# A chunk inverse whose first transposed step is made by a mask on VectorE

## The chip, the cores and the metric

The kernel runs on one core of a Trainium2 chip. The metric is the device time of one execution in microseconds (us), the median of the runs shown. PE is the matrix engine (TensorE), PEld its weight loads, DVE is VectorE, ACT is ScalarE, POOL is GpSimd, and SP issues the weight transfers. Times in the rows are counted from the start of the profiled span.

## The reference, cut to what matters

One inference step of a two-layer decoder trunk runs over 512 prompt tokens and 8 samples of 8 tokens. Each layer has a mixer (one combined input projection; a gated delta rule with 4 heads of 128, a pooling and a short convolution read it), an output projection, and a gated MLP. In the delta rule each chunk of tokens needs a triangular solve:

```
a = einsum('bhnid,bhnjd->bhnij', kb, k) * where(strict, decay, 0)
sol = lax.linalg.triangular_solve(eye + a, rhs, left_side=True, lower=True)
u, w = sol[..., :dv], sol[..., dv:]
```

The kernel takes four chunks of 128 prompt tokens (0 to 3) and one block-diagonal chunk of 64 rows for all samples (chunk 4), and builds the inverse of `eye + a` for all 4 heads of a chunk.

## The kernel before, in words

Tokens stand in the free dimension (576 of them, in two halves of 288 columns), features on partitions. A dense matmul multiplies a 128x128 weight piece by one half. Each fp32 product is made of three matmuls of rounded parts (`xh` by `whi`, `xl` by `whi`, `xh` by `wlo`); ACT makes `whi` from the loaded `wraw`, DVE makes `wlo`. The input projection of a layer has 24 groups of 48 dense matmuls, 1152 in all; this text counts places on PE by how many of them have gone before. The delta rule runs inside the projection, between its dense matmuls, from the 444th on.

The order is written once, when the program is built. Generators (`tri`, `delta`, `sample`, `vtrans` and the tails of each group) are advanced by a planner that keeps an estimated clock for each engine; `tick`, after each three dense matmuls, advances those whose estimated front has passed. `aside` marks work on which the generator's front does not wait. On the chip every engine then runs its own list in that order and waits on semaphores. `room(2)`, at the start of each group, advances generators until at most two tails still hold a PSUM bank. The pooling tails wait for `vtrans`, the transposes of V, so that at place 864, the start of the group after the two pooling groups, the planner writes out all that `vtrans` needs and whatever comes up meanwhile, with no dense matmul between.

`tri` inverts a chunk. Two streams of it run side by side: stream 0 has chunks 0 and 2, stream 1 has 1, 4 and 3. It builds `A` (fp32) from the cumulated gates `gc` and the products of K (`KQ` rows on PE), its fp16 copies `Ah` and `Al`, and the factor `E`. Then it doubles the inverse, 7 steps for 128 rows and 3 for 64. `UT[:, :, 0]` is the inverse so far, `UT[:, :, 1]` its transposed form. A step s multiplies `Ah` with the inverse (P, 4 matmuls), masks P by level s (H, one DVE operation), multiplies H with the transposed form both ways (Y, 8 matmuls in two PSUM banks) and copies both banks with ACT. In step 0 the inverse is the identity, so P is a transpose through `identr`. Two refinement rounds and the product with Q follow.

In rows `m` and `m_149` to `m_152` are the four memory regions that hold these tiles: `UT` of stream 0 lies in `m_151`, that of stream 1 and `Ah`, `Al`, `H` in `m_152`, `A` and `U` in `m_149`. A row `ps<-m` or `ps<-m,m` with f16 is a matmul of `tri`; `vs<-ps,c` is ACT copying a V transpose, `cv`, `pad` and `VZ<-th,cv` are the convolution tails of K, Q and V.

Of the kernel before, what the change touches and what calls it, by code (L numbers as in the profile page):

```python
# [10 lines left out]
F16 = mybir.dt.float16  # L11
I32 = mybir.dt.int32
AF = mybir.ActivationFunctionType
ALU = mybir.AluOpType
# [8 lines left out]
NH = 4  # L23
# [16 lines left out]
    _C[_n] = (_o, _o + _w)  # L40
    _o += _w
NCONST = _o
NLEV = 7 * 128
_P = {}
_o = 0
for _n, _w in (("gmix", 8), ("gffn", 8), ("gfin", 8), ("cw", 48), ("alog", 20), ("dtb", 20), ("onorm", 1),
# [6 lines left out]
def _levels():  # L53

    i = np.arange(128)
    lev = np.zeros((128, 7, 128), np.float32)
    for n in range(7):
        b = i >> n
        lev[:, n] = np.eye(128) - ((b[:, None] // 2 == b[None, :] // 2) & (b[:, None] % 2 == 0) & (b[None, :] % 2 == 1))
    return lev.reshape(128, NLEV)  # L60


def _constants():
    c = np.zeros((128, NCONST + NLEV), np.float32)
    c[:, NCONST:] = _levels()

    def put(n, a):
        a = np.asarray(a, np.float32)
        c[:a.shape[0], _C[n][0]:_C[n][0] + a.shape[1]] = a

    i = np.arange(128)
    put("ident", np.eye(128))
    put("ones", np.ones((128, 2)))
    put("tu", i[:, None] <= i[None, :])
    s = np.arange(64)
    blk = (s[:, None] // ST) == (s[None, :] // ST)
    put("tus", blk & (s[:, None] <= s[None, :]))
    put("bones", blk)
    put("mx", np.where(i[:, None] > i[None, :], -1e30, 1e4))
    put("my", np.where(i[None, :] >= i[:, None], 1e30, -1e4))  # L80
    put("mxs", np.where(blk & (s[:, None] > s[None, :]), -1e30, 1e4))
    put("mys", np.where(blk & (s[None, :] >= s[:, None]), 1e30, -1e4))
    put("bmask", (s[:, None] // ST) == np.arange(8)[None, :])
    put("sel", np.tile(np.eye(8), (2, 1)))
    win = np.repeat(np.array([[2, 4], [8, 16]]), 64, axis=1).T
    put("winv", 1.0 / win)
    put("wsel", np.repeat(np.array([[0, 1], [0, 1]]), 64, axis=1).T)
    pos = np.arange(15)
    put("ptab", np.concatenate([1.0 / np.minimum(pos[None, :] + 1, win[:, t:t + 1]) for t in range(2)], axis=1))
    return c  # L90
# [150 lines left out]
class _Trunk:  # L241
# [933 lines left out]
    def tri(self, l, par, chunks):  # L1175

        nc, V, S = self.nc, self.nc.vector, self.nc.scalar

        def tl(name, dt=F32):
            return self.carve(f"{name}{par}", (NH, 128), dt)  # L1180

        for c in chunks:
            n = 128 if c < 4 else 64
# [3 lines left out]
            idr = self.identr[0:n, 0:n]  # L1187
# [7 lines left out]
            def grid(p=n):  # L1195
                return self.psum()[0:p, 0:NH * n].rearrange("p (h i) -> p h i", i=n)
# [23 lines left out]
            with self.aside():  # L1220
                if c < 4:
                    V.tensor_copy(ekv, B[:, :, 127:128])
                    V.tensor_tensor(out=ek[:, NH:2 * NH], in0=ek[:, 0:NH], in1=self.gc[:, 4 * c:4 * c + NH],
                                    op=ALU.subtract)
# [15 lines left out]
            Ah = tl("Ah", F16)[0:n, :, 0:n]  # L1240
# [14 lines left out]
            lev = self.lev[0:n]  # L1255
            UT = self.carve(f"UT{par}", (NH, 2, 128), F16)[0:n, :, :, 0:n]
            for s in range(7 if c < 4 else 3):
                P = grid()
                for h in range(NH):
                    self.mm(P[:, h], Ah[:, h], idr if s == 0 else UT[:, h, 0])  # L1260
                H = UT[:, :, 0] if s == 0 else tl("H", F16)[0:n, :, 0:n]
                V.tensor_tensor(out=H, in0=P, in1=lev[:, s:s + 1, 0:n].to_broadcast([n, NH, n]), op=ALU.mult)
                self.back(P)
                yield
                if s == 0:
                    Y = grid()
                    for h in range(NH):
                        self.mm(Y[:, h], H[:, h], idr)
                    S.activation(out=UT[:, :, 1], in_=Y, func=AF.Copy)
                    self.back(Y)  # L1270
                else:
                    for j in (0, 2):
                        Y = self.psum()[0:n, 0:4 * n].rearrange("p (h u i) -> p h u i", u=2, i=n)
                        for i in range(2):
                            self.mm(Y[:, i, 0], UT[:, j + i, 1], H[:, j + i])
                            self.mm(Y[:, i, 1], H[:, j + i], UT[:, j + i, 1])
                        with self.aside():
                            S.activation(out=UT[:, j:j + 2], in_=Y, func=AF.Copy)
                            self.back(Y)
                yield  # L1280

            if c in (2, 3):
                yield lambda: len(self.chunks) > c - 2 and self.chunks[c - 2]
# [4 lines left out]
            for it in range(2):  # L1288
                P = grid()
                for h in range(NH):  # L1290
                    self.mm(P[:, h], Ah[:, h], C[:, h], stop=False)
                    self.mm(P[:, h], Al[:, h], C[:, h], start=False)
                F = tl("H", F16)[0:n, :, 0:n]
# [319 lines left out]
    def build(self):  # L1613
        nc, tc, ctx, a = self.nc, self.tc, self.ctx, self.a
        V, S = nc.vector, nc.scalar
# [57 lines left out]
        nc.gpsimd.dma_start(out=self.const[:, c0:], in_=a["consts"][:, c0:NCONST])  # L1673
        levels = [self.temp("lev") for _ in range(2)]
        self.free["tmp"] -= 2
        for j, (s0, s1) in enumerate(((0, 4), (4, 7))):
            nc.gpsimd.dma_start(out=levels[j][:, 0:128 * (s1 - s0)],
                                in_=a["consts"][:, NCONST + 128 * s0:NCONST + 128 * s1])

        def halve():  # L1680

            self.lev = self.pc.tile([128, 7, 128], F16, name="lev")
            V.tensor_copy(self.identr, self.c("ident"))
            for j, (s0, s1) in enumerate(((0, 4), (4, 7))):
                V.tensor_copy(self.lev[:, s0:s1], levels[j][:, 0:128 * (s1 - s0)].rearrange("p (s i) -> p s i", i=128))
            self.give(*levels)

# [24 lines left out]
        for l in range(L):  # L1712
            name, _, groups = next(ph)
# [437 lines left out]
```

## Time and profile before

| | us |
|---|---|
| median of 3 runs (1498.53 to 1500.83) | 1499.11 |
| the profiled execution's own time | 1498.7 |
| its span | 1496.9 |

The span is from the first to the last instruction; 1.8 us lie around it. PE is busy for 1467.6 us of the span, so little of it is spent waiting, and what waits there are can be listed one by one.

### The profile page before, as it was taken

How to read it: one execution, taken by the hardware profiler on the slowest of the kernel's cores; microseconds unless marked ns; L12 is line 12 of the kernel's file. 1: busy time of each engine (PE TensorE's matmuls, PEld its weight loads, DVE VectorE, ACT ScalarE, POOL GpSimd, SP SyncE). 2: the span in 40 equal slices, each digit the busy share in tenths (PEclk: the TensorE clock that was granted, in tenths of full speed). 3: DMA queues.
4: the chain of work that ended last, by engine and by line, in shares of the span. 5: the costliest groups of instructions: out<-in, count | busy, mean ns of one | idle time of the engine just before them, and what ended most of it. 6: DMA issues, size and time to landing. Idle time of an engine off the chain costs nothing.

```text
span 1496.9 us, 29634 instructions
## 1 busy us (share of the span) xinstructions
PE 1467.6 (98%) x11462; PEld 1430.1 (96%) x11462; DVE 1072.3 (72%) x2381; ACT 670.2 (45%) x1427; POOL 186.9 (12%) x636
## 2 busy tenths in 40 slices
PE   9999999999999999999999999999999999999997
PEld 7999899899999999999999988989999999999997
DVE  7887776668748786478667887766595678854865
ACT  6345565544433343144434546755343334432442
POOL 3211023401000010001121111242010001000100
PEclk9999999999999999999999999999999999999999
DMA  6121122332232323222422112025222232232222
GB/s 199 58 63 44 48 75 86 129 103 78 85 92 86 99 72 92 85 93 73 144 75 70 58 43 90 26 86 174 78 78 79 84 102 82 85 92 92 72 84 85
DMA packets 67278, 128.78 MB, mean 86 GB/s; under 512 B 7952, under 2 KB 13248, under 8 KB 67136
## 3 DMA queue, kind: packets, MB, share of 16 engines
q1 hardware_dynamic: 59808, 105.15, 22.7%
q0 software_dynamic: 6208, 20.56, 3.8%
q8 instruction: 90, 1.47, 0.4%
q10 hardware_dynamic: 1120, 1.18, 0.2%
q14 instruction: 52, 0.43, 0.1%
HBM read 116.36 MB, written 10.49 MB: 85 GB/s over the span
## 4 chain that ended last, share of the span: by engine, by line
PE 87%; issue 5%; DVE 4%; POOL 2%; ACT 1%; DMA 1%; SPq 0%; POOLq 0%; DVEq 0%; ACTq 0%
PE ps L458 75%; PE q L458 10%; PE ps L229 2%; DVE m L229 1%; DMA xr<-in_x_dram 1%; ACT m L229 1%; DVE cv L229 1%; DVE wlo L229 0%; DVE sqacc L229 0%; POOL kr_t L229 0%; POOL os_t L229 0%; POOL qr_t L229 0%; ACT whi L229 0%; POOL o_y L229 0%; DVE xl L229 0%
## 5 line engine op out<-in xcount | busy, mean ns | idle before, releaser
L229 DVE TENSOR_TENSOR wlo<-wraw,whi 128x512 fp32r<-128x512 f32 (+1 forms) x428 | 285.7, 677 | 84.1 <-ACT whi L229 82.6
L229 ACT ACTIVATE whi<-wraw 128x512 fp32r<-128x512 f32 (+1 forms) x428 | 257.1, 615 | 147.3 <-PE ps L458 122.1
L458 PE MATMUL ps<-xh,whi 128*128 128x288 f32 x768 | 243.7, 317 | 0.1
L458 PE MATMUL ps<-xl,whi 128*128 128x288 f32 x768 | 227.1, 296 | 0.5 <-DVE xl L229 0.5
L458 PE MATMUL ps<-xh,wlo 128*128 128x288 f32 x768 | 226.4, 295 | 0.4 <-DVE wlo L229 0.4
L458 PE MATMUL ps<-hh,whi 128*128 128x288 f32 x704 | 208.5, 296 | 0.0
L458 PE MATMUL ps<-hl,whi 128*128 128x288 f32 x704 | 207.6, 295 | 0.0
L458 PE MATMUL ps<-hh,wlo 128*128 128x288 f32 x704 | 207.0, 294 | 0.0
L458 PE MATMUL ps<-nh,whi 128*128 128x288 f32 x640 | 189.3, 296 | 0.0
L458 PE MATMUL ps<-nl,whi 128*128 128x288 f32 x640 | 188.8, 295 | 0.0
L458 PE MATMUL ps<-nh,wlo 128*128 128x288 f32 x640 | 188.2, 294 | 0.0
L458 PEld LDWEIGHTS ps<-xh,whi 128*128 128x128 f32 x768 | 144.7, 188 | 5.8 <-issue 2.4
L458 PEld LDWEIGHTS ps<-xl,whi 128*128 128x128 f32 x768 | 144.9, 189 | 1.5 <-DVE xl L229 1.1
L458 PEld LDWEIGHTS ps<-xh,wlo 128*128 128x128 f32 x768 | 144.5, 188 | 0.9 <-DVE wlo L229 0.9
L458 PEld LDWEIGHTS ps<-hh,wlo 128*128 128x128 f32 x704 | 132.6, 188 | 0.0
L458 PEld LDWEIGHTS ps<-hl,whi 128*128 128x128 f32 x704 | 132.2, 188 | 0.0
L458 PEld LDWEIGHTS ps<-hh,whi 128*128 128x128 f32 x704 | 131.9, 187 | 0.0
L458 PEld LDWEIGHTS ps<-nh,wlo 128*128 128x128 f32 x640 | 120.5, 188 | 0.0
L458 PEld LDWEIGHTS ps<-nl,whi 128*128 128x128 f32 x640 | 120.1, 188 | 0.0
L458 PEld LDWEIGHTS ps<-nh,whi 128*128 128x128 f32 x640 | 119.9, 187 | 0.0
L229 POOL COPY fs<-gpad 128x2 f32<-128x2 f32 x88 | 30.7, 365 | 677.2 <-DVE gpad L229 604.5
L229 DVE SCALAR_TENSOR_TENSOR xr<-ps,xr 128x288 f32<-128x288 f32 x96 | 41.2, 457 | 99.5 <-PE ps L458 99.1
(312 smaller groups left out, 3354.3 us busy)
## 6 DMA issues: line engine op xcount, KB each, us to landing
wraw<-in_w_gu_dram SPq DMA_DIRECT2D x176, 256.0 KB, 2.8
wraw<-in_w_in_dram SPq DMA_DIRECT2D x96, 256.0 KB, 2.7
wraw<-in_w_dn_dram SPq DMA_DIRECT2D x80, 256.0 KB, 2.7
wraw<-in_w_out_dram SPq DMA_DIRECT2D x32, 256.0 KB, 2.9
xr<-in_x_dram POOLq DMA_DIRECT2D x12, 288.0 KB, 5.3
vs<-in_st_delta_dram POOLq DMA_DIRECT2D x6, 512.0 KB, 4.4
out_s_delta_dram<-vs POOLq DMA_DIRECT2D x6, 512.0 KB, 3.1
spill<-xr POOLq DMA_DIRECT2D x8, 288.0 KB, 2.5
```

The source lines that it names most:

```text
L229: return f(*args, **kw)
L458: self.nc.raw.tensor.matmul(out, lhsT, rhs, start=start, stop=stop)
```

## The change: the diff and the new order

A further level, `lev[:, 7]`, is the transpose of level 0. In step 0 the change makes `UT[:, :, 1]`, which was the transpose of the masked H, directly as `Ah` times this level, by one DVE operation on fp16 from SBUF. The four second transposes, the PSUM bank they took and ACT's copy go, and with them the `yield` that followed. The constants grow by 128 columns, which come with the second of two transfers.

```
     for n in range(7):
         ...
+    lev[:, 7] = lev[:, 0].T
...
                 P = grid()
+                if s == 0:
+                    with self.aside():
+                        V.tensor_tensor(out=UT[:, :, 1], in0=Ah, in1=lev[:, 7:8, 0:n].to_broadcast([n, NH, n]),
+                                        op=ALU.mult)
                 for h in range(NH):
                     self.mm(P[:, h], Ah[:, h], idr if s == 0 else UT[:, h, 0])
                 H = UT[:, :, 0] if s == 0 else tl("H", F16)[0:n, :, 0:n]
                 V.tensor_tensor(out=H, in0=P, in1=lev[:, s:s + 1, 0:n].to_broadcast([n, NH, n]), op=ALU.mult)
                 self.back(P)
                 yield
-                if s == 0:
-                    Y = grid()
-                    for h in range(NH):
-                        self.mm(Y[:, h], H[:, h], idr)
-                    S.activation(out=UT[:, :, 1], in_=Y, func=AF.Copy)
-                    self.back(Y)
-                else:
+                if s:
                     for j in (0, 2):
...
-                yield
+                    yield
```

Since the planner's clocks see other costs, the order of the whole mixer changes in both layers. The first place is DVE in layer 0, where chunks 0 and 1 end (`m_150<-ps,m_149` is their product with Q) and chunks 2 and 4 begin (`ps,gc`). Before, from place 711 on PE:

```order
L229 TENSOR_TENSOR m_149<-m_149,ps 128x512
L229 TENSOR_TENSOR m_149<-m_152 128x512
L229 TENSOR_TENSOR m_152<-m_150,ps 128x512
L229 TENSOR_TENSOR m_150<-ps,m_149 128x512
L229 TENSOR_TENSOR m_149<-m_149,ps 128x512
L229 SCALAR_TENSOR_TENSOR m_149<-ps,gc,consts 128x128 x4
L229 COPY ek<-ps 128x4
L229 TENSOR_TENSOR ek<-ek,gc 128x4
L229 TENSOR_TENSOR m_150<-ps,m_149 128x512
L229 SCALAR_TENSOR_TENSOR m_149<-ps,beta,m_149 128x128 x4
L229 TENSOR_TENSOR m_149<-m_149,consts 128x512
L229 SCALAR_TENSOR_TENSOR m_149<-ps,gc,consts 64x64 x4
```

Now, from place 768 to 777:

```order
L230 TENSOR_TENSOR m_149<-m_149,ps 128x512
L230 SCALAR_TENSOR_TENSOR cv<-pad,prm_91,cv 128x600 x3
L230 TENSOR_TENSOR pad<-ps,rn 128x288
L230 TENSOR_TENSOR pad<-ps,rn 128x224
L230 TENSOR_TENSOR pad<-ps,rn 128x8x8
L230 TENSOR_TENSOR wlo_2130<-wraw_1820,whi_2129 128x512
L230 TENSOR_TENSOR m_149<-m_149,ps 128x512
L230 TENSOR_TENSOR m_150<-ps,m_149 128x512 x2
L230 SCALAR_TENSOR_TENSOR m_149<-ps,gc,consts 128x128 x4
L230 COPY ek<-ps 128x4
L230 TENSOR_TENSOR ek<-ek,gc 128x4
L230 SCALAR_TENSOR_TENSOR m_149<-ps,gc,consts 64x64 x4
```

A convolution, a group's evacuation and a weight split now stand ahead of the beginning of chunk 2, and that beginning has moved 66 dense matmuls later. On PE the first transpose of chunk 2 moves from place 750 to 813, that of chunk 4 from 786 to 864.

The second place is ACT in layer 0 at place 864, where the V transposes are copied (`vs<-ps,c`) between the copies of the doubling steps (`m_151<-ps` for chunk 2, `m_152<-ps 64x4x64` for chunk 4). Before:

```order
L229 ACTIVATE m_152<-ps 64x4x64 x2
L229 ACTIVATE m_151<-ps 128x512 x2
L229 ACTIVATE m_152<-m_150 64x4x64
L229 ACTIVATE vs<-ps,c_1007 64x128 x4
L229 ACTIVATE m_152<-ps 64x4x64
L229 ACTIVATE m_151<-ps 128x512 x2
L229 ACTIVATE vs<-ps,c_1007 128x128 x4
L229 ACTIVATE m_151<-ps 128x512 x2
L229 ACTIVATE vs<-ps,c_1007 128x128 x8
L229 ACTIVATE m_149<-m_149 128x512
L229 ACTIVATE ek<-ek 128x8
L229 ACTIVATE m_151<-ps 128x512 x2
```

Now:

```order
L230 ACTIVATE vs<-ps,c_1007 64x128 x4
L230 ACTIVATE m_151<-ps 128x512 x2
L230 ACTIVATE m_152<-ps 64x4x64 x2
L230 ACTIVATE vs<-ps,c_1007 128x128 x4
L230 ACTIVATE m_151<-ps 128x512 x2
L230 ACTIVATE m_152<-ps 64x4x64 x2
L230 ACTIVATE vs<-ps,c_1007 128x128 x4
L230 ACTIVATE m_152<-m_150 64x4x64
L230 ACTIVATE m_151<-ps 128x512 x2
L230 ACTIVATE vs<-ps,c_1007 128x128 x4
L230 ACTIVATE m_152<-ps 64x4x64
L230 ACTIVATE m_151<-ps 128x512 x2
```

Chunk 2 now has its first five doubling steps' Y products in this stretch, where it had four of later steps, and chunk 4 has both its doubling steps and its refinement there. Layer 1 has the same order as layer 0 in both places.

## Rows read from the trace of the kernel before

**Rows 1.** The page, parts 1 and 4: busy time of each engine; the chain's shares.

```profile
PE 1467.6 (98%) x11462; PEld 1430.1 (96%) x11462; DVE 1072.3 (72%) x2381; ACT 670.2 (45%) x1427; POOL 186.9 (12%) x636
...
PE 87%; issue 5%; DVE 4%; POOL 2%; ACT 1%; DMA 1%; SPq 0%; POOLq 0%; DVEq 0%; ACTq 0%
```

**Rows 2.** Timeline, PE: start, duration, engine, line, operation, shapes, [idle before].

```profile
143.68 0.38 PE L458 MATMUL ps<-m 128*128 128x128 f16 x4 [1.27 <-ACT m L229]
...
282.98 0.40 PE L458 MATMUL ps<-ol,whi 128*128 128x288 f32 x1 [1.25 <-DVE ol L229]
...
869.90 0.61 PE L458 MATMUL ps<-m 128*128 128x128 f16 x8 [0.52 <-DVE m L229]
...
880.97 0.38 PE L458 MATMUL ps<-m 128*128 128x128 f16 x4 [1.70 <-ACT m L229]
```

**Rows 3.** Stretches: length, busy PE, PEld, DVE, ACT, POOL; clock, DMA, GB/s.

```profile
175.20:187.80 12.60, 9.75 (x117) 8.19 (x116) 7.79 (x22) 10.22 (x30) 0.00 (x0) 1.00 0.02 6
...
912.40:925.10 12.70, 9.85 (x119) 8.22 (x117) 7.90 (x23) 10.22 (x30) 0.00 (x0) 1.00 0.03 10
```

**Rows 4.** Groups by form, PE, ACT and DVE: count, busy us, mean ns, idle.

```profile
L458 PE MATMUL ps<-identr,m 128*128 128x128 f16 x64 | 6.3, 221 | 0.0
...
L229 ACT ACTIVATE m<-ps 128x512 f16<-128x512 f32 x112 | 60.0, 599 | 33.9 <-PE ps L458 33.9
...
L229 ACT ACTIVATE m<-ps 64x256 f16<-64x256 f32 x12 | 4.1, 375 | 6.6 <-PE ps L458 4.0 <-issue 2.6
...
L229 DVE TENSOR_TENSOR m<-ps,lev 128x512 f16<-128x512 f32 x56 | 37.9, 686 | 10.1 <-PE ps L458 9.9
```

**Rows 5.** Tile lev: the casts of the levels, ns min, median, max.

```profile
L229 DVE CAST lev<-lev x2: 352/385/418, 28.5 to 28.8; 128x512 f16<-128x512 f32 x1, 128x384 f16<-128x384 f32 x1
```

**Rows 6.** Timeline, PE: a group of 4 and one of 8 between dense matmuls.

```profile
134.81 0.29 PE L458 MATMUL ps<-xh,wlo 128*128 128x288 f32 x1
...
134.95 0.40 PE L458 MATMUL ps<-m 128*128 128x128 f16 x4
...
135.37 0.30 PE L458 MATMUL ps<-xl,whi 128*128 128x288 f32 x1
...
137.21 0.29 PE L458 MATMUL ps<-xh,wlo 128*128 128x288 f32 x1
...
137.35 0.62 PE L458 MATMUL ps<-m 128*128 128x128 f16 x8
...
137.99 0.30 PE L458 MATMUL ps<-xl,whi 128*128 128x288 f32 x1
```

**Rows 7.** Timeline around the beginning of chunk 2, PE, DVE and ACT.

```profile
131.87 1.28 DVE L229 TENSOR_TENSOR m<-ps,lev 128x512 f16<-128x512 f32 x2
...
133.67 2.60 DVE L229 SCALAR_TENSOR_TENSOR cv<-pad,prm,cv 128x600 f32<-128x600 f32 x3
...
146.82 1.06 PE L458 MATMUL ps<-KQ 128*128 128x128 f32 x8
...
148.74 1.12 DVE L229 SCALAR_TENSOR_TENSOR m<-ps,gc,consts 128x128 f32<-128x128 f32 x4
...
154.50 0.61 ACT L229 ACTIVATE m<-m 128x512 f16<-128x512 f32 x1
```

**Rows 8.** Timeline inside the stretch at place 864.

```profile
175.04 1.56 DVE L229 SCALAR_TENSOR_TENSOR VZ<-th,cv 128x512 f32<-128x512 f32 x4
...
176.48 0.69 PE L229 MATMUL ps<-consts,VZ 128*64 128x128 f32 x4
...
178.29 0.61 PE L458 MATMUL ps<-m,m 128*128 128x128 f16 x8 [0.47 <-DVE m L229]
...
180.90 0.61 PE L458 MATMUL ps<-m,m 128*128 128x128 f16 x8 [0.41 <-DVE m L229]
...
181.38 1.08 ACT L229 ACTIVATE m<-ps 128x512 f16<-128x512 f32 x2 [0.55 <-PE ps L458]
182.35 1.15 ACT L229 ACTIVATE vs<-ps,c 128x128 f32<-128x128 f32 x4
```

**Rows 9.** Stretches of 1 us in layer 0, the clock behind POOL's time.

```profile
124.00:125.00 1.00, 1.00 (x11) 0.97 (x11) 0.98 (x6) 0.87 (x2) 0.00 (x0) 0.74 0.00 0
...
126.00:127.00 1.00, 1.00 (x12) 1.00 (x12) 1.00 (x3) 0.36 (x1) 0.00 (x0) 0.50 0.00 0
127.00:128.00 1.00, 1.00 (x10) 1.00 (x9) 1.00 (x4) 1.00 (x3) 0.00 (x0) 0.55 0.00 0
```

More of the change, by code (lines that the diff above doesn't have):

```diff
@@ L42 @@
 NCONST = _o
-NLEV = 7 * 128
+NLEV = 8 * 128
 _P = {}
@@ L55, in _levels @@
     i = np.arange(128)
-    lev = np.zeros((128, 7, 128), np.float32)
+    lev = np.zeros((128, 8, 128), np.float32)
     for n in range(7):
@@ L1675, in build @@
         self.free["tmp"] -= 2
-        for j, (s0, s1) in enumerate(((0, 4), (4, 7))):
+        for j, (s0, s1) in enumerate(((0, 4), (4, 8))):
             nc.gpsimd.dma_start(out=levels[j][:, 0:128 * (s1 - s0)],
@@ L1680, in halve @@
         def halve():
-            self.lev = self.pc.tile([128, 7, 128], F16, name="lev")
+            self.lev = self.pc.tile([128, 8, 128], F16, name="lev")
             V.tensor_copy(self.identr, self.c("ident"))
-            for j, (s0, s1) in enumerate(((0, 4), (4, 7))):
+            for j, (s0, s1) in enumerate(((0, 4), (4, 8))):
                 V.tensor_copy(self.lev[:, s0:s1], levels[j][:, 0:128 * (s1 - s0)].rearrange("p (s i) -> p s i", i=128))
```

## The prediction, made before the changed kernel ran

> **What bounds it now.** I read the page first: PE is busy for 1467.6 of 1496.9 us and carries 87% of the chain that ended last; DVE stands at 72%, ACT at 45% [rows 1]. So a microsecond saved on DVE or ACT counts only where PE waits for it, and a microsecond taken off PE counts in full where the next thing PE needs is there in time. Next the list of PE's waits. In a layer they are few, and all belong to the mixer: 1.27 us at the end of chunks 0 and 1, where PE waits for ACT's copy of a half of the inverse (in layer 0; 0.52 and 1.70 in layer 1), the waits inside the stretch at place 864, and 1.25 us for `ol` at its end [rows 2]. That stretch lasts 12.60 us in layer 0 and 12.70 in layer 1, has no dense matmul, and PE is busy for 9.75 and 9.85 of it [rows 3]. Both ACT (10.22) and PE are well filled there, DVE less (7.79). Last the clock: from 124 to 128 in layer 0, after a run of small matmuls, it is at 0.50, the 1.2 GHz level, for some 0.52 + 1 + 1 + 0.9 = 3.4 us (a slice at 0.74 was half slow) [rows 9]. At half speed 3.4 us do 1.7 us of work, so it costs 1.7.
>
> **What is removed.** Per layer four chunks of 128 rows and one of 64 lose a group of 4 fp16 matmuls. Between the dense matmuls at 134.81 and 135.37 stand one dense matmul and a group of 4: 0.56 less two pitches. From 135.37 to 137.21 there are ten pitches and a group of 8; the group of 8 by the second pair of rows (137.21 to 137.99, two pitches again) is 0.78 less two pitches. Both together give a pitch of 0.133 and 0.29 and 0.51 for the groups [rows 6]. Ten groups come to 2.1 us if each goes at the second half of a group of 8 (0.21), 3.0 at 0.30; the two with 64 rows are smaller, so I take 8 x 0.30 + 2 x 0.1 = **2.6 us**. ACT loses 8 copies of 599 ns and 2 of 375 [rows 4], 5.5 us, off PE's path wherever PE has dense matmuls.
>
> **What is added.** Ten DVE operations, eight of 128x512. No row of before multiplies fp16 by fp16 from SBUF. The nearest from below is the cast to fp16 of the same size, 0.352 to 0.418 us [rows 5]; from above the product with a level out of PSUM, 0.686 [rows 4]. I take 0.6, since it has two operands as the latter; the bounds differ by 0.27 us an operation. The Trainium skill's *VectorE: DVE Perf Modes*, section "Mode 2×_1P — pack two bf16 into one 32-bit read", has 16-bit operands of step 1 go at two results a cycle; by it the cost would be at the cast's end, an estimate of 0.42, and the sum would be smaller by 0.2 for each such operation in PE's way. It is ahead of H on DVE, so H is late by it only if it is still running when P is there. Where dense matmuls lie between (42 of them in chunk 0, 42 x 0.133 = 5.6 us, against 0.6 for `Al`, 1.1 for E, 0.69 and 0.69: 3.1), the cover is 2.5 us, and it costs nothing. Without cover, as for chunk 4 inside the stretch, it costs its length. The 64 KB of constants land with the others before the levels are cast at 28.5 us [rows 5], long ahead of the mixer's first chunk; nothing waits.
>
> **What is moved.** This decides the sum. The order of before has the tail of chunks 0 and 1 at place 711 and the transpose of chunk 2 at 750, of chunk 4 at 786. Now the tail is at 768 to 777, the transpose of chunk 2 at 813 and that of chunk 4 at 864. The old waits at the tail then go: 1.27 + 0.52 + 1.70 = **3.5 us** [rows 2]. The stretch of small matmuls that led to the slow clock is cut up too, since the tail comes later; I take the **1.7** as gained, with nothing as its other end.
>
> New waits come. From place 768 on DVE must do, before `Ah` of chunk 2 is ready: a convolution triple (2.60), about seven operations of 512 (0.65 each, 4.6), two groups of gate and decay operations (1.12 each), one of 64 rows (0.8), pads and small ones (about 1.1); then comes ACT's `Ah` (0.61) [rows 4, 7]. That is 12.0 us, and four hand-overs between PE and DVE, which cost PE 0.4 to 0.5 each where it waits for DVE now [rows 8], bring it to about 13.9. PE has meanwhile 45 pitches (6.0), five or six groups of 4 (1.7 to 2.0) and the cluster of `KQ` and `gc` products (1.06 a full group, three and a half of them with two `gc` groups, some 4.1) [rows 6, 7]: 12.0. So PE waits **1.9 us** before the transpose of chunk 2, in before hidden behind 31 dense matmuls and more (`Ah` by 155.1 [rows 7]). The refinement at 768 to 777 has its own waits of about 0.8, since the convolution and the weight split stand between its two DVE steps. Together 2.7 a layer, **5.4**. What bounds this: if all 512-wide operations go at the cast's 0.42 the list is 1.6 shorter and the wait 0.3; if each hand-over is 0.3 longer it is 3.1.
>
> **The stretch at 864.** In before, the V tail (`VZ<-th,cv`) is done by 176.6, when the first V transposes start 1.3 us into it [rows 8], and chunk 2 is in its later steps; `KQ` and `gc` products of chunk 3 fill holes. Now all of steps 1 to 5 of chunk 2, steps and refinement of chunk 4, and the V transposes stand there. A step is P, H on DVE, two Y groups and ACT's copies, and the next P needs the copies. In before two steps stand 178.29 to 180.90 apart, 2.61 [rows 8], with ACT holding V copies (1.15 for four) between two Y copies (1.08) [rows 8]. I lay it out: DVE's list from 768 to the V tail is 21 us (two triples 5.2, twelve of 512 7.8, three groups of 1.12, two of 64 rows 1.6, VZ 1.6, the rest 1.5) [rows 4, 7, 8] against 18.9 on PE (96 pitches 12.8, fp16 groups 2.0, the cluster 4.1), so part of the 2.1 is already paid at 813 and V comes about 1 us late. First Y at 2.5 us, the second at 7.3 (the late V and the start of chunk 4), three more at 2.75 each (2.61 and chunk 4's added operation in part), 0.45 to the end: **16.0 us**, and 3.4 a layer above before, **6.8**. The work in it hardly changes (two doubling steps' fp16 groups and chunk 4's beginning come in, about 1.9; the `KQ` and `gc` groups, about as much at 1.06 a full group [rows 7], moved behind it). Bounds: 12.6, if V and chunk 4 fall in the holes of the steps; 19, if each of five steps takes 3.3 with ACT in between.
>
> Behind it chunk 3 starts at 894 in place of 891, with chunk 2's end crowded at 867 to 879: 0 to 2 us a layer, I take 0.8, **1.6**. The waits at the end of the mixer [rows 2] have almost the same order and stay.
>
> **Sum.** −2.6 −3.5 −1.7 +5.4 +6.8 +1.6 = +6.0. The profiled execution took 1498.7, 1.8 outside its span, and the median of before is 0.4 above; so 1504.7, or **1505 us**. A measurement of this kernel tells 0.2%, 3.0 us, from no change: "same" is 1496.1 to 1502.1.
>
> **Rivals.** *Traded evenly (1496).* V and chunk 4 fit the holes, the stretch stays at 12.6 and chunk 3 is not late: −2.6 −3.5 −1.7 +5.4 = −2.4, 1496.3. For it: net work in the stretch is unchanged and ACT has lost a copy for each chunk. Against it: five steps in a row cannot be shorter than five times a chain of P, H, Y and copies, and before had four.
>
> *Faster (1491).* DVE is not behind at place 768 and catches up: if it is 2 us or more ahead of my count there, `Ah` is ready at 813 and V at 864, and nothing replaces the old waits: −2.6 −3.5 −1.7 = −7.8, 1490.9. It decides as soon as the 512-wide operations take 0.5 and not 0.65. For it: DVE stands idle 28% of the span [rows 1]. Against it: the operation of the refinement at 768 cannot start before PE's product, so no earlier idle time is carried over.
>
> *Slow clock (1508 to 1512).* PE idles in short bits for 16 us in the stretch. In before the clock there stays at 1.00 in both layers [rows 3], but small matmuls did bring it to 0.50 [rows 9]. If it falls once per layer for 3.4 us, +1.7 each: 1508.4; if the chain's PE work (about 0.70 a step, five steps) goes at half, +3.5 each: 1512. The Trainium skill's *TensorE: Matmul & The Clock Gate*, section "A second HAM failure mode: psum-queue depth-cycling", says that short idle times of PE between groups of matmuls can make the clock swing between half and full; the stretches of before, with the same short waits at full clock, don't bear it out so far.
>
> *The added operation delays H everywhere:* 8 x 0.6 = 4.8 without any cover. The 2.5 us of cover speak against it; it is inside the slower cases.
>
> **Chances.** My sum 0.40, slow clock 0.18, traded evenly 0.24, faster 0.18. Faster by over 0.2% 0.20 (the lower edge of the even case falls under 1496.1), same 0.23, slower 0.57. The forecast's own range is 1502 to 1511; for 8 in 10 it must reach down past the even case to half of the faster one and up to the slow clock: 1491 to 1514.
>
> **What the changed profile would show.** 40 fewer matmuls; no wait on ACT at the end of chunks 0 and 1; a wait of 1 to 3 us on ACT `m` before the `identr` group at 813; waits on DVE at the first V transposes; the stretch between dense matmuls at 864 near 16 us in both layers; the DVE product with `lev` from SBUF at 0.4 to 0.7. I am wrong if `Ah` is ready at 813, if the stretch is 13 us or below, or if the clock in it falls below 0.9. What would move the whole outside the range is a wait at a place that I count as unchanged, the end of the mixer above all.

## The result, and the profile after

The changed kernel takes 1546.48 us (median of 4 runs, 1541.85 to 1546.81) against 1498.92 us before: a ratio of 1.0308 (of the means), 95% interval 1.0296 to 1.0321. That is 47.6 us more, eight times the 6 us that were forecast and far outside the range. The profiled execution took 1541.85 us; the other three took 1546.4 to 1546.8 at a mean clock of 0.973 against its 0.978, so what is added up below from its trace comes to 43.2 us and not to 47.6.

The page of the changed kernel, its busy times, the granted clock in 40 slices, and the shares of the chain that ended last:

```profile
PE 1488.7 (97%) x11422; PEld 1446.6 (94%) x11422; DVE 1074.6 (70%) x2391; ACT 664.2 (43%) x1417; POOL 181.1 (12%) x636
...
PEclk9999799999999999999999997899999999999998
...
PE 80%; DVE 8%; issue 5%; ACT 3%; POOL 2%; DMA 1%; SPq 0%; POOLq 0%; DVEq 0%; ACTq 0%
```

The span is 1540.1 us. PE has 40 matmuls fewer than in [rows 1] and yet is busy for 21.1 us more, and its idle time (span less busy) has gone from 29.3 to 51.4. Three slices, in the mixers of the two layers, show a lower clock. The next views take them apart. First all stretches of the changed kernel, and the one of before, in which the clock stands at half while PE has work; the last microseconds of both, when PE has next to none, are left out (columns: length, busy PE, PEld, DVE, ACT, POOL, clock, DMA, GB/s):

```profile
175.70:196.10 20.40, 17.45 (x136) 14.36 (x137) 8.76 (x23) 13.49 (x38) 1.95 (x7) 0.50 0.07 22
220.00:223.40 3.40, 3.40 (x23) 3.08 (x21) 3.27 (x9) 0.88 (x2) 0.00 (x0) 0.51 0.00 0
933.40:953.90 20.50, 18.06 (x136) 15.43 (x136) 7.50 (x16) 13.06 (x37) 2.35 (x7) 0.50 0.12 35
960.70:971.00 10.30, 10.30 (x51) 9.79 (x50) 2.93 (x6) 3.90 (x10) 1.21 (x3) 0.50 0.05 15
981.20:984.60 3.40, 3.40 (x24) 3.19 (x23) 2.91 (x8) 0.46 (x1) 0.00 (x0) 0.50 0.01 2
sum 58.00, PE 52.61 PEld 45.84 DVE 25.36 ACT 31.79 POOL 5.51; mean PE 10.52 PEld 9.17 DVE 5.07 ACT 6.36 POOL 1.10
```

```profile
124.50:127.90 3.40, 3.40 (x26) 3.24 (x27) 3.08 (x10) 2.12 (x5) 0.00 (x0) 0.50 0.00 0
```

PE was busy for 52.6 us at 1.2 GHz, which at 2.4 GHz is 26.3 us of work; before, 3.4 us, 1.7. So the slow clock costs **24.6 us** more than before. The rest of PE's busy time has fallen by 24.6 − 21.1 = **3.5 us**. That is a remainder, put down to the removed groups, which were forecast at 2.6 within 2.1 to 3.0; the changed operations in the order of before, the kernel e1 below, give 3.6 by the same count (1467.6 − 1.7 against 1465.7 − 3.4; e1 has 6.8 us at half clock). The waits give **22.1 us**. Together 24.6 + 22.1 − 3.5 = 43.2, the difference of the two spans.

Where PE waits, from the list of its waits (sum, times, longest), before and then now, and from the timeline of layer 0 around places 765 to 777, 813, 864, 876 and 894:

```profile
PE ps L458 <- ACT m L229: 3.7, 4, 1.7
PE ps L458 <- DVE m L229: 3.0, 7, 0.5
```

```profile
PE ps L459 <- DVE m L230: 18.8, 20, 3.5
PE ps L459 <- ACT m L230: 6.5, 10, 1.9
PE ps L230 <- DVE VZ L230: 2.9, 2, 1.4
```

```profile
149.25 0.38 PE L459 MATMUL ps<-m 128*128 128x128 f16 x4 [0.45 <-ACT m L230]
150.74 0.61 PE L459 MATMUL ps<-m 128*128 128x128 f16 x8 [0.19 <-ACT m L230]
153.11 0.38 PE L459 MATMUL ps<-m,m 128*128 128x128 f16 x4 [1.77 <-DVE m L230]
154.50 0.38 PE L459 MATMUL ps<-m 128*128 128x128 f16 x4 [0.16 <-DVE m L230]
...
165.77 0.40 PE L459 MATMUL ps<-identr,m 128*128 128x128 f16 x4 [0.50 <-ACT m L230]
...
175.74 0.85 PE L230 MATMUL ps<-consts,VZ 128*64 128x128 f32 x3 [1.45 <-DVE VZ L230]
...
202.97 2.05 PE L459 MATMUL ps<-m,m 128*128 128x128 f32 x16 [1.88 <-ACT m L230]
218.60 0.38 PE L459 MATMUL ps<-m 128*128 128x128 f16 x4 [3.46 <-DVE m L230]
```

The tail of chunks 0 and 1 waits as it did [rows 2], in another place and for 0.45 + 0.19 + 1.77 + 0.16 = 2.57 us; the first V transposes wait for the V tail; chunk 3's second step waits longest. What DVE does ahead of that wait:

```profile
215.16 0.69 DVE L230 TENSOR_TENSOR wlo<-wraw,whi 128x512 fp32r<-128x512 f32 x1 [1.19 <-ACT whi L230]
215.77 0.68 DVE L230 TENSOR_TENSOR m<-m,m 128x512 f16<-128x512 f32 x1
216.49 1.13 DVE L230 SCALAR_TENSOR_TENSOR m<-ps,gc,consts 128x128 f32<-128x128 f32 x4
217.53 0.42 DVE L230 TENSOR_TENSOR m<-m,lev 128x512 f16<-128x512 f16 x1
217.86 0.68 DVE L230 TENSOR_TENSOR m<-ps,lev 128x512 f16<-128x512 f32 x1
```

H (the last row) stands behind `Al`, E and the added product, 2.2 us of work, with no dense matmul between P and the next P. Only 0.42 of it is new; and ahead of all of them stands a weight split that has itself waited 1.19 us for ACT. The clock in relation to the waits, layer 0:

```profile
170.00:173.00 3.00, 3.00 (x23) 2.87 (x22) 2.96 (x8) 0.75 (x2) 0.00 (x0) 1.00 0.00 0
173.00:176.00 3.00, 1.18 (x12) 0.74 (x11) 2.52 (x6) 1.82 (x4) 0.00 (x0) 0.94 0.20 64
176.00:196.00 20.00, 17.10 (x135) 14.03 (x134) 8.36 (x23) 13.49 (x38) 1.85 (x7) 0.50 0.06 18
196.00:199.00 3.00, 3.00 (x28) 2.87 (x27) 1.15 (x3) 1.02 (x5) 0.52 (x1) 0.98 0.84 309
...
216.00:220.00 4.00, 1.40 (x14) 1.33 (x14) 3.96 (x9) 1.12 (x2) 0.00 (x0) 1.00 0.20 66
220.00:223.00 3.00, 3.00 (x22) 2.93 (x21) 2.87 (x8) 0.48 (x1) 0.00 (x0) 0.51 0.00 0
```

The clock falls right behind the two slices in which PE is busy for 1.18 of 3 us and 1.40 of 4, and after the first of them it stays down for as long as the run of small matmuls lasts, and 2.3 us more. A wait does not always bring it: the 1.77 us at 153.11 and the 1.88 at 202.97 are followed by full clock. Nor is a wait needed: the one fall of before, at 124.5, came after 29.5 us in which PE was busy throughout:

```profile
95.00:124.50 29.50, 29.50 (x280) 28.43 (x279) 26.70 (x57) 17.91 (x33) 3.83 (x12) 1.00 0.20 64
```

The stretch of [rows 3], 12.60 us at full clock before, is 20.80 here, at a mean clock of 0.57 (its row stands with the filled kernel's below).

### The profile page after: what moved, and what is told of

Read it like the earlier page. It is cut to its first block, busy times and chain, and to the rows that moved or that the text cites. A ratio compares the mean times of both kernels' runs of the same rounds, so it can differ in the third digit from the quotient of the medians.

```text
span 1540.1 us, 29586 instructions
## 1 busy us (share of the span) xinstructions
PE 1488.7 (97%) x11422; PEld 1446.6 (94%) x11422; DVE 1074.6 (70%) x2391; ACT 664.2 (43%) x1417; POOL 181.1 (12%) x636
## 3 DMA queue, kind: packets, MB, share of 16 engines
q10 hardware_dynamic: 1120, 1.18, 0.2%
## 4 chain that ended last, share of the span: by engine, by line
PE 80%; DVE 8%; issue 5%; ACT 3%; POOL 2%; DMA 1%; SPq 0%; POOLq 0%; DVEq 0%; ACTq 0%
PE ps L459 68%; PE q L459 10%; DVE m L230 3%; PE ps L230 2%; ACT m L230 2%; DVE cv L230 1%; DVE wlo L230 1%; DMA xr<-in_x_dram 1%; ACT whi L230 1%; DVE VZ L230 1%; POOL o_t L230 1%; POOL os_t L230 0%; DVE sqacc L230 0%; POOL kr_t L230 0%; DVE vs L230 0%
```

## The experiments

The theory after this reading: the operations of the change cost nothing; the order that the planner writes once its costs are changed makes all of the loss, by waits and through them by the clock. The rivals: the operations themselves delay the chains (the product with the added level stands ahead of H), or the slow clock comes from the small matmuls whatever waits there are.

**Operations and order apart.** Two kernels cross them. In the first the planner is charged for the old step and not for the new one; in the second the other way round.

```diff
# e1: changed operations, order of before      # spends: planner's clock alone
-                    with self.aside():
-                        V.tensor_tensor(out=UT[:, :, 1], in0=Ah, in1=lev[:, 7:8, ...
+                    V.eng.tensor_tensor(out=UT[:, :, 1], in0=Ah, in1=lev[:, 7:8, ...
...
+                if s == 0:
+                    self.phantom(NH, n)     # a bank, 4 matmuls, a copy: spends only
# e2: operations of before, order of the change
+                    with self.aside():
+                        self.spend("vector", ...)       # the added product
...
-                        self.mm(Y[:, h], H[:, h], idr)
-                    S.activation(out=UT[:, :, 1], in_=Y, func=AF.Copy)
+                        self.nc.raw.tensor.matmul(Y[:, h], H[:, h], idr, start=True, stop=True)
+                    S.eng.activation(out=UT[:, :, 1], in_=Y, func=AF.Copy)
```

> The operations of the change (no second transposes, no copy, the product with the added level) in the order of before: each engine's list is that of before without the removed rows and with the ten added ones. If the order made the loss: 1498.9 less the 2.6 us of the ten groups, less up to 2 us if the shorter run of small matmuls in layer 0 moves the slow clock, so 1494 to 1498. If the operations themselves made it (the DVE product in front of H, or fewer PE columns in a stretch): 1520 or more, with half clock in the stretch at place 864.

> The operations of before (second transposes, copy, no added product) in the order of the change: each list is that of the changed kernel with the old rows in place of the ten new ones. If the order made the loss: 1546 and 1 to 6 us more for the groups and the copies, 1545 to 1553, with some 20 us of half clock at place 864 in each layer. If the operations made it: 1499 to 1505.

| | order of before | order of the change |
|---|---|---|
| operations of before | 1498.92 | 1546.25; ratio 1.0306 (1.0292 to 1.0320) |
| operations of the change | 1497.32; ratio 0.9983 (0.9974 to 0.9992) | 1546.48; ratio 1.0308 (1.0296 to 1.0321) |

Each ratio is to the runs of before on the same chip (1499.8 for the two crossed kernels). The order makes the loss, with either set of operations; the operations in the old order gain 2.5 us (1.2 to 3.9 by the interval), which is what was expected of the removed groups. In the new order no difference between the two sets shows, but the two ratios leave some 3 us either way, so that a gain of 2.5 us there is not excluded. Between e1 and the changed kernel, which have the same operations, the traces give 20.5 us more of waiting (30.9 and 51.4) and 22.9 more for the clock (3.4 and 26.3). The stretch at place 864 of the first crossed kernel answers to [rows 3], unchanged in length and busy time:

```profile
175.10:187.70 12.60, 9.75 (x118) 8.19 (x117) 7.80 (x22) 10.22 (x30) 0.00 (x0) 1.00 0.01 4
```

**The cast alone (e4).** The added level also makes the planner's cost of a cast larger, and that moves rows well ahead of the mixer.

```diff
-                V.tensor_copy(self.lev[:, s0:s1], ...)
+                self.spend("vector", _Engine.FIXED["vector"] + 512 * _Engine.WORD["vector"])
+                V.eng.tensor_copy(self.lev[:, s0:s1], ...)
```

> Before, with only the planner's cost of the second cast of levels raised from 384 to 512 columns (0.13 us on its VectorE clock). Nine rows of PE's list move, all before the mixer. The part of the change's loss that lies before place 444 is 1.0 us: 1499.5 to 1500.5 if these rows made it and nothing later follows; 1510 or more if the planner's order is so loose that any small cost ends in the bad order.

Measured 1499.65 us, ratio 0.9998 (0.9989 to 1.0007): no part of the loss.

**Filling the wait that stands ahead of the slow clock (e6).** PE gets work at the first V transposes, which the transposes overwrite.

```diff
             vc = self.carve("vc", (4, 128), F32, 5, "X")
+            if c == 4:
+                for _ in range(12):
+                    nc.raw.tensor.matmul(ps[:, 0:128], self.c("ident"), self.c("ident"), start=True, stop=True)
```

> The changed kernel with 12 further fp32 matmuls of constants (1.5 us, overwritten by what follows) ahead of the first V transposes at place 864 in both layers, where PE waits 1.45 us for DVE; all other rows stand as in the changed kernel. If that wait is what lets the clock fall, the stretch runs at full clock: it shortens from 21.1 us to 15.5 to 17 in both layers, and the time is 1533 to 1538. If it is the small matmuls and short waits inside the stretch that hold the clock down, whatever stands at its beginning, the clock falls a little later and the time is 1543 to 1549.

Measured 1535.97 us, ratio 1.0244 (1.0229 to 1.0259), 10.5 us less than the changed kernel by the medians. That is the first range, but only one layer does what this range assumed. The stretch at place 864 of layer 0 in the changed kernel, and then in this one, followed by a slice inside it in layer 0, the same slice in layer 1, and what comes behind that one:

```profile
172.95:193.75 20.80, 16.08 (x133) 12.91 (x132) 9.93 (x25) 13.83 (x40) 0.00 (x0) 0.57 0.09 26
```

```profile
172.50:189.40 16.90, 13.30 (x158) 11.29 (x156) 9.66 (x24) 13.13 (x39) 0.00 (x0) 1.00 0.11 32
...
177.14:180.64 3.50, 2.26 (x28) 1.82 (x27) 1.48 (x5) 3.50 (x13) 0.00 (x0) 1.00 0.03 6
932.50:936.00 3.50, 2.28 (x28) 1.82 (x27) 1.46 (x5) 3.50 (x13) 0.00 (x0) 1.00 0.00 0
936.00:953.00 17.00, 15.50 (x113) 13.37 (x113) 6.42 (x15) 9.83 (x27) 2.36 (x7) 0.50 0.16 55
```

In layer 0 the clock stays at 1.00 and the stretch is 3.9 us shorter, though the 12 matmuls took longer than I had reckoned: in the timeline of this kernel they are, in layer 0 and as long in layer 1,

```profile
173.47 2.94 PE L1335 MATMUL ps<-consts 128*128 128x128 f32 x24
```

with two records to a matmul, 2.94 us and not 1.5, so that they outlast the wait of 1.45 by about that much. At full clock the stretch would be 16.90 − 1.5 = 15.4 us, an estimate. In layer 1 the same work keeps the clock up at the V transposes only: it falls a few microseconds later, at 936.0, behind a slice of small matmuls and short waits in which PE is busy for 2.28 of 3.50 us. The same slice in layer 0, with PE busy for 2.26 of 3.50, is followed by full clock. So neither the wait at the beginning nor the small matmuls behind it decide by themselves, and what does stays open.

Nor is the gain simply that stretch. The traced execution of this kernel took 1540.65 us, 1.2 less than that of the changed kernel (its other executions took 1534.1 to 1536.6), and the clock stands at half in it almost as long, in part in places where it did not before (154.4 to 157.8, 198.7 to 209.0 and 908.7 to 912.1 among them):

```profile
sum 51.10, PE 49.24 PEld 45.96 DVE 27.51 ACT 17.48 POOL 6.24; mean PE 6.16 PEld 5.75 DVE 3.44 ACT 2.18 POOL 0.78
```

That is 24.6 us for the clock, against 26.3 in the changed kernel.

**Filling all three long waits**, with more matmuls (e7) and then with fewer (e12):

```diff
+                if c == 3 and s == 1:                  # in tri, into P
+                    for _ in range(24):                # second kernel: 15
+                        nc.raw.tensor.matmul(P[:, 0], self.c("ident"), self.c("ident"), start=True, stop=True)
...
+            if c == 0:                                 # in delta, into ds
+                for _ in range(14):                    # second kernel: 8; V transposes 12, then 6
+                    nc.raw.tensor.matmul(ds[:, 0], ident, ident, start=True, stop=True)
```

> The changed kernel with overwritten fp32 matmuls of constants in the three longest waits of each layer: 12 at the first V transposes (wait 1.45 us), 14 ahead of the products with vp of chunk 0 (1.88), 24 ahead of the first P of chunk 3's second step (3.46). All other rows stand. If these waits alone let the clock fall, there is full clock from place 864 on in both layers, and of the 58 us at half clock nearly all go: 1546.5 less 20 to 25, so 1521 to 1527, and what is left above before (some 24 us) is PE waiting. If small matmuls by themselves hold the clock down: 1535 to 1545, as with the first of the three places alone (1536) or worse by the work added.

> As with all three places filled, but with 6, 8 and 15 matmuls for 12, 14 and 24: the trace of the first filled kernel has 12 of them take 2.9 us, 0.23 us each and not 0.12, so that the three groups outlasted their waits by 1.3, 1.3 and 2.0 us in each layer. If only that kept the gain small: 1539.7 less 9.2, 1529 to 1533. If the smaller fill lets the clock fall again in layer 1 and more: 1536 to 1546.

Measured 1539.65 us, ratio 1.0277 (1.0261 to 1.0293), and 1542.68 us, 1.0288 (1.0272 to 1.0303). Both miss the theory's number and lie in the range of the rival. But the edit does not do all that was meant. The matmuls into `ds` stand behind the wait of 1.88 us and not in it, in the second kernel too; only the other two places are filled. In the first kernel, layer 0:

```profile
197.29 3.39 PE L1435 MATMUL ps<-consts 128*128 128x128 f32 x28 [1.87 <-ACT m L230]
212.44 5.58 PE L1266 MATMUL ps<-consts 128*128 128x128 f32 x48
```

In its layer 0 the clock is full from 155.6 on, through the stretch at place 864 and both places behind; in layer 1 the stretch falls to half as in the kernel before. This is its row, and the sum of all four stretches at half clock:

```profile
933.80:950.90 17.10, 15.32 (x113) 13.19 (x112) 6.69 (x15) 10.10 (x28) 2.37 (x7) 0.50 0.15 47
...
sum 27.30, PE 25.37 PEld 22.94 DVE 15.34 ACT 10.10 POOL 3.52; mean PE 6.34 PEld 5.73 DVE 3.84 ACT 2.52 POOL 0.88
```

So the clock costs 12.7 us in place of 26.3, PE's idle time falls by 13.0 to 38.4 us, and the filling adds 2 × (2.94 + 3.39 + 5.58) = 23.8 us of work, which takes nearly all of it back. In the second kernel, with half as many matmuls at the V transposes, the stretch of layer 0 falls to half too (from 177.7 to 198.2), and the mean clock is 0.981. What the waits cost beside the clock can't be got apart by these two kernels.

**H first, in the order of the change (e8).** On DVE the added product, `Al` and E go behind H of step 0; the planner's clocks and all other lists are kept.

```diff
+            def later():
+                V.eng.tensor_tensor(out=UT[:, :, 1], in0=Ah, in1=lev[:, 7:8, ...), op=ALU.mult)
+                V.eng.tensor_tensor(out=Al, in0=A, in1=Ah, op=ALU.subtract)
+                ...                                    # E: four operations, and ACT's Exp
...
                 V.tensor_tensor(out=H, in0=P, in1=lev[:, s:s + 1, 0:n].to_broadcast([n, NH, n]), op=ALU.mult)
                 self.back(P)
+                if s == 0:
+                    later()
```

> The changed kernel with DVE's list altered in step 0 alone: H stands ahead of the product with the added level, of Al and of E's four operations, where it stood behind them; PE's and ACT's lists are the same. If the added product and its neighbours delay H where there is no dense matmul to hide them, PE's wait of 3.46 us at chunk 3 shortens by 0.42 + 0.68 + 1.13 = 2.2 us in each layer, and the fall of the clock behind it may go too (1.7 each): 1538 to 1543. If H is late for another reason (the ones that feed DVE, ACT's copy to fp16): 1545 to 1548.

Measured 1547.69 us, ratio 1.0324 (1.0310 to 1.0338), no gain. The timelines of PE and ACT at chunk 3 show why:

```profile
221.38 0.38 PE L459 MATMUL ps<-m 128*128 128x128 f16 x4 [1.37 <-DVE m L230]
224.96 4.21 PE L459 MATMUL ps<-m,m 128*128 128x128 f32 x20 [3.20 <-ACT m L230]
```

```profile
223.79 0.63 ACT L1261 ACTIVATE m<-m 128x512 f32<-128x512 f32 x1 [3.79 <-DVE m L1259]
224.33 0.58 ACT L230 ACTIVATE m<-ps 128x512 f32<-128x512 f32 x1
```

The wait for H is 1.37 us in place of 3.46, 2.1 less where 2.2 were expected. So the time lies in the second range, but not for the reason given there, that H is late all the same. ACT's list still has E's Exp ahead of the copy `m<-ps` that PE's next products need. E comes later from DVE now, ACT waits 3.79 us for it with the copy queued behind, and PE waits 3.20 us for the copy. The time moved from one queue to the next.

**H first, in the order of before (e9):**

> The operations of the change in the order of before, and H ahead of the added product, Al and E on DVE. If in this order dense matmuls hide all of these, as the prediction had it for the cover: as without this edit, 1497.3 with 1 us either way. If the added product stood in PE's way somewhere: 0.4 to 2 us less.

Measured 1497.90 us, ratio 0.9990 (0.9981 to 0.9999), against 0.9983 (0.9974 to 0.9992) without the edit: no difference that shows. So the added product costs nothing that can be measured in that order.

**Other orders.** Four orders with the operations of the change: the planner charged for neither step (e10), for both (e11), and the changed kernel with the two inverse streams allowed to start earlier or later (e13, e14).

```diff
-        "square": -0.6, "update": 0.35, "v": -0.45, "vtrans": -0.05, "zgate": 0.75}
+        "square": -0.6, "update": 0.35, "tri0": -0.2, "tri1": -0.2, "v": -0.45, ...   # e14: 0.2
```

> The changed operations, with the planner told of neither the old step (matmuls and copy) nor the added product: a third order, with 128 small matmuls at place 864 where before has 108 and the changed kernel 132. If any order but the one that the kernel's table of waits was written for loses much: 1515 to 1550. If the changed kernel's order is an unlucky one: 1494 to 1503.

> The changed operations, with the planner told of the old step and of the added product: a fourth order, chunk 2 at 771 and 136 small matmuls at place 864. If the number of small matmuls in that place decides: 1535 to 1550, as the changed kernel (132). If the start of chunk 2 decides: between before (750) and the changed kernel (813), 1505 to 1530.

> The changed kernel with one pair of numbers added to the planner's table of waits: both inverse streams may start work 0.2 us before their estimated front. The order then has chunk 2's first transpose at 738 (before 750, changed kernel 813), and fewer than 24 small matmuls at place 864, spread over 843 to 861. If the order makes the loss and the operations cost nothing: 1495 to 1510, no half clock over 10 us in a layer. If the operations themselves cost: over 1530.

> The same pair of numbers at +0.2: the streams start late, chunk 2's first transpose at 825, chunk 3's at 945, 44 small matmuls at place 864 and runs of 25 to 36 behind. If the long run at place 864 is what costs, through the clock: 1500 to 1520, although the streams are later still. If their lateness costs, whatever stands at 864: 1540 to 1560.

| | time, us | ratio (95%) | span less PE busy, us | mean clock |
|---|---|---|---|---|
| before | 1498.92 | | 29.3 | 0.996 |
| e1, order of before | 1497.32 | 0.9983 (0.9974 to 0.9992) | 30.9 | 0.996 |
| changed kernel | 1546.48 | 1.0308 (1.0296 to 1.0321) | 51.4 | 0.978 |
| e10, neither cost | 1529.92 | 1.0205 (1.0191 to 1.0219) | 53.4 | 0.988 |
| e11, both costs | 1526.36 | 1.0179 (1.0153 to 1.0205) | 47.8 | 0.987 |
| e13, streams early | 1534.72 | 1.0235 (1.0220 to 1.0250) | 49.1 | 0.982 |
| e14, streams late | 1532.45 | 1.0217 (1.0202 to 1.0233) | 50.5 | 0.988 |

Each ratio is to the runs of before on the same chip (medians 1498.92 to 1499.92); the last two columns are from the traced execution. In every other order PE waits 18 to 24 us more than in that of before, and is busy for 1477.7 to 1488.7 us, 12 to 23 above the 1465.7 of e1 with the same work: the clock. e10 came out in its first range and e11 in its second; e13 lies in the range for operations that cost by themselves, which e1 had ruled out, and e14 between its two. Three numbers that I took for the measure of an order do not decide: e11 has the most small matmuls at place 864 (136) and is the fastest of the five new orders, e13 has the fewest there and of the five the earliest chunk 2, and is the second slowest, so its expectation failed; and e14, with the streams latest, is faster than the changed kernel. What moves is which wait is long: in e10 one is for the load of the delta rule's state (`vs`, 4.0 us in layer 0; e11 has it too), in e13 it is ACT (`m` and `ms`), in e14 DVE (`m`, and `VZ`):

```profile
PE ps L474 <- DMA vs<-in_st_delta_dram: 6.2, 2, 4.0
```

```profile
PE ps L459 <- ACT m L230: 9.4, 9, 2.2
PE ps L230 <- ACT ms L230: 8.9, 4, 3.2
```

```profile
PE ps L459 <- DVE m L230: 16.2, 8, 3.1
PE ps L230 <- DVE VZ L230: 7.2, 2, 3.6
```

## Why the prediction was wrong

The direction was right, and so was the ground for it: what is moved decides, not what is removed or added. The size was wrong by a factor of eight. The forecast sum was +6.0, the traced execution's span grew by 43.2; of the 37.2 between, 26.3 are the clock (+24.6 where the forecast had −1.7), 11.8 the waits (+22.1 where it had −3.5 +5.4 +6.8 +1.6 = +10.3), and −0.9 the removed groups. By its steps:

- **Removed: −2.6.** Nearly right: 3.5 us of PE's work went, above the 3.0 of the upper bound, and 2.5 us of time where the order is kept.
- **Added: 0.6 an operation, no cost under cover.** The operation takes 0.415 us (0.271 with 64 rows), at the cast's end of the bounds. The Trainium skill's *VectorE: DVE Perf Modes*, section "Mode 2×_1P — pack two bf16 into one 32-bit read", has two results a cycle for 16-bit operands, which had given the estimate of 0.42; the trace agrees. In the order of before it costs nothing that shows (e9). In the new order the cover was missing: the prediction worked it out for chunk 0, but chunk 3 at place 894 has no dense matmul there, and `Al`, E and the product stand ahead of H.
- **Old waits gone: −3.5.** They went from their old places, but the tail of chunks 0 and 1 waits for 2.57 us a layer in its new place, where the forecast had 0.8. The slow clock of before at 124.5 is gone in the changed kernel, as forecast, but that is no success of the forecast: it is gone as well in the kernel with the cast alone, whose order there is that of before and which has its slow clock at 187.3, and in e1 and e9, which have theirs in layer 1 (at 862.2 and 923.6, and at 860.7).
- **New waits at 768 to 813: 2.7 a layer.** 2.57 + 0.43 + 0.50 = 3.5, 0.8 more and not in the forecast's places: the wait at 813 is 0.50 and not 1.9, and the one that I gave 0.8 is 2.57. That the longer waits at 765 to 777 gave DVE the time that I had it lack at 813 is likely and not shown.
- **The stretch at 864: 16.0.** Right as a count of work and hand-overs, about 15.4 at full clock by the filled kernel. But it ran at half clock for 18 of its 20.80 us in layer 0. **This is the step that failed:** I took the clock as 1.00, on the ground that the stretch of before ran at 1.00 with the same short waits [rows 3], and I had myself forecast a late V at its beginning without asking what that wait does to the clock. PE was busy for 17.45 us at half clock from there on in layer 0 and for 18.06 in layer 1; half of that, 17.8 us, is what the step left out.
- **Behind it: 0.8 a layer.** Wrong, and the larger part of what the waits were missed by: 1.88 us at place 876 and 3.46 at 894, 5.3 in place of 0.8, and further falls of the clock behind them (3.4 us at half clock in layer 0, 10.3 and 3.4 in layer 1).
- **The slow-clock rival (0.18, 1508 to 1512).** It names the larger of the two mechanisms, but its price, 3.4 to 7 us in all, was four to eight times too low: 26.3 us were lost. I priced the one fall of before, 3.4 us, or the chain's PE work alone. On the chip the clock stayed down for 20.4 us, through all of the run of small matmuls, with everything that PE does there. I had set it aside since the stretch of before did not show it. The Trainium skill's *TensorE: Matmul & The Clock Gate*, section "A second HAM failure mode: psum-queue depth-cycling", tells of a kernel in which short idle times between groups made the clock swing. The trace after agrees with it in part: five stretches at half clock, 58 us, each in or behind the waits; but the fall of before came with PE busy throughout, and the same slice with the same waits fell in one layer of e6 and not in the other.

What is shown: the order carries the loss whatever operations stand in it (e1, e2), the loss is waits (22.1 us) and clock (24.6) in the traced execution, and with the wait at the V transposes filled the stretch of layer 0 kept its full clock in the two traces that have this (e6 and e7). That waits start the slow clock is likely from this, and not shown: in layer 1 the same filling did not keep it up. What stays open: what makes the clock fall in one layer and not in the other, and which property of an order makes it good. None that I could read from the lists ahead of a run foretold the times of e10 to e14, and how much of the waits would remain at full clock was not got apart.

The version that beats both kernels, by a little, is the change in the order of before, 0.9983 (0.9974 to 0.9992).

## What to carry to other kernels

Where a planner with estimated clocks writes the order of a whole stage, an edit changes two things, the operations and the order; cross the two before judging either. Here the operations are worth −2.5 us and the order +47. To keep an order, charge the planner for what was there and issue what is new. And where an edit leaves PE a wait next to a run of small matmuls, count among the rivals that the clock stays down for the whole run, and not for the wait alone.

## What the runs showed of the hardware that was not expected

One wait of 1.45 us, with PE busy for 1.18 of 3 us around it, was followed by 20.4 us at 1.2 GHz; in e2, the same order with the operations of before, by 13.7. One fall came with no wait at all (before, at 124.5), and the same matmuls with the same short waits ran at full clock in one layer and at half in the other (e6, e7). While the clock is down, PE was busy for 52.6 of 58.0 us, so a busy engine is no sign that its clock is up. An fp32 matmul of 128x128 leaves two records in the trace and takes 0.23 to 0.25 us (24 records in 2.94 us, 48 in 5.58). A DVE product of fp16 by fp16 from SBUF takes 0.415 us for 512 columns, against 0.685 with one operand in PSUM and fp32:

```profile
L230 DVE TENSOR_TENSOR m<-ps,lev x62: 405/685/693, 100.2 to 1007.0; 128x512 f16<-128x512 f32 x56, 64x256 f16<-64x256 f32 x6
L230 DVE TENSOR_TENSOR m<-m,lev x10: 271/415/417, 99.9 to 978.9; 128x512 f16<-128x512 f16 x8, 64x256 f16<-64x256 f16 x2
```
